# Mixture-of-experts stage on one core: the smallest expert group's rows in four 32-column tiles of TensorE instead of two of 64

## The chip, the core and the metric

The kernel runs on one core of a Trainium2 chip. The metric is the device time of one execution in microseconds. Before the change it is 1832.76 us, the median of 3 runs (1832.09 to 1835.33).

## What is computed

Two layers of a transformer-like trunk over 512 frames of width 1024. Each layer has a mixing half (three kinds of attention between one input and one output projection) and a mixture-of-experts half; the change lies in the second. All of it is float32. The part that matters, cut from the reference:

```python
h2 = rms_norm(x) * (1 + sc2) + sh2            # 512 x 1024
scores = sigmoid(h2 @ router_w)               # 32 experts in 8 groups of 4
g_sel = argmax over groups of (sum of the best two biased scores of a group)
idx, gates = the best two experts inside the group g_sel
for each of a token's two experts e:
    u = silu(h2 @ w_gate[e]) * (h2 @ w_up[e])      # 1024 -> 512
    y += gate * (u @ w_down[e])                    # 512 -> 1024
x = x + gt2 * y
```

A token stays inside one group, so a group is a list of tokens, and each of the 32 experts reads the list of its group. With these inputs the routing formulas put 115, 96, 85, 71, 54, 46, 31 and 14 tokens into the eight groups of the first layer (sorted), and 108, 105, 94, 64, 50, 41, 30 and 20 in the second.

## The kernel before

**Places.** The groups are ranked by count (lines 1276 to 1288). Rank r gets `CAPS[r]` places in a gathered activation `hs` (lines 1363 to 1376): 128 for ranks 0 to 3 ("wide"), 64 for ranks 4 to 7 ("narrow"), 768 in all. A one-hot matrix `Pt` (line 1310) is multiplied with the activations (line 1370, 2 halves of 384 places, 8 slices of the width, 8 matmuls each), and each result goes through DVE (line 1374) or ACT (line 1376) into `hs`. Tokens beyond a group's places would go through a loop behind the stage (lines 1686 on) that is skipped when there are none.

**Weights.** Each expert has 6 MB in fp32 (gate, up and down), fetched by SP in pieces of 1 MB (line 1447) into 8 buffers of 1 MB; a buffer comes free when its last reader is done, and SP, which issues in order, waits for that. 192 such transfers make the stage of one layer.

**Wide experts.** ACT casts each half of a piece to a rounded fp32r high part and DVE subtracts to get the low part (`split`, lines 1415 to 1424). TensorE runs three fp32r matmuls of 512 columns for each product (`three`).

**Narrow experts.** No split: plain fp32 matmuls straight from the fetched piece. An fp32 matmul is two passes on TensorE, each a MATMUL with its weight load. With only 64 rows to produce, `halved` puts the first half of the output columns on array columns 0 to 63 (PSUM partitions 0 to 63) and the second half on 64 to 127; the two column tiles run at the same time. A gate or up part is 8 slices x 2 halves x 256 columns, a down part 4 slices x 2 halves x 512 columns. `up_part` folds the halves back with two DVE operations that read every second element, `turn` transposes.

**Order.** `WHERE` alternates a wide rank and a narrow one, in four quarters: ranks 0 and 4, 1 and 5, 2 and 6, 3 and 7; the last four experts are (3,2), (3,3), (7,2), (7,3). The engines' order is written out (`_Pinned`): gate of expert e+1, with the transposes of expert e in the middle, down of e, up of e+1. ACT's casts are put into its queue up to four half pieces ahead of the matmul that reads them. Behind the last expert of a group its sums are gated with gt2 and scattered back to the 512 rows by matmuls with `PT` and DVE adds into `X` (`add`); `combine` does this in steps between the pieces of the next experts, `combine_last` does it for rank 7 at the end of the stage, with nothing behind it but the next layer's start (squares and row norm), or in the second layer the output's store. For a narrow group `add` reads the two column halves of the sums as two row tiles of 64.

In the trace nearly all of this has line 122, the helper that pins the order; tiles tell the parts apart: `g`, `u` and `y` are the sums of gate, up and down, `R` the fetched piece, `H` its split, `x` a scratch bank.

Of the kernel before, what the change touches and what calls it, by code (L numbers as in the profile page):

```python
# [12 lines left out]
F32R = mybir.dt.float32r  # L13
# [3 lines left out]
OP = mybir.AluOpType  # L17
# [10 lines left out]
START = GV, DQ, DK  # L28

NWIDE = 4  # L30
CAPS = (128,) * NWIDE + (64,) * (NG - NWIDE)
OFFS = tuple(sum(CAPS[:r]) for r in range(NG))
PLACES = sum(CAPS)

# [105 lines left out]
def hybrid_trunk(ctx: ExitStack, tc: tile.TileContext, x, c, positions, w_mod, b_mod, norm1_g, norm2_g, w_in,  # L140
# [228 lines left out]
    for l in range(depth):  # L369
        first = l == 0  # L370
        with ExitStack() as ps:
# [900 lines left out]
            def pt_(shape):  # L1272
                return p3.tile(shape)
# [17 lines left out]
            nth, rk, aw, cap, over, slot = [pt_([128, NT]) for _ in range(6)]  # L1291
            V.tensor_mul(tmp.rearrange("p i g -> p (i g)"), pc[:, 0:NT * NG], gf)
            V.tensor_tensor(tmp2, grp, rank[:, None, :].to_broadcast([128, NT, NG]), op=OP.mult)
            V.tensor_reduce(nth, tmp, axis=AX.X, op=OP.add)
            V.tensor_reduce(rk, tmp2, axis=AX.X, op=OP.add)
            V.tensor_scalar(cap, rk, NWIDE - 0.5, CAPS[-1] - CAPS[0], op0=OP.is_gt, op1=OP.mult)
            V.tensor_scalar(aw, rk, float(NWIDE), 0.0, op0=OP.subtract, op1=OP.max)
            V.tensor_scalar(cap, cap, float(CAPS[0]), None, op0=OP.add)
            V.scalar_tensor_tensor(aw, aw, CAPS[-1] / CAPS[0] - 1.0, rk, op0=OP.mult, op1=OP.add)
# [49 lines left out]
            def pre_done():  # L1349

                spre.close()
                pre.clear()
                wn = after["pool"] = pool(spre, f"wn{l}", "right")
                after["gt2b"] = wn.tile([128, D])
                A.dma_start(after["gt2b"], bcast(mods[l, 5 * D:6 * D], D))
                after["gt2h"] = wn.tile([128, 512])
                for n in range(2):
                    A.dma_start(after["gt2h"][64 * n:64 * n + 64], bcast(mods[l, 5 * D + 512 * n:5 * D + 512 * n + 512], 512, 64))

            def pbank(tag, bufs=1, shape=None):  # L1360
                return pm.tile(shape or [128, 512], tag=tag, bufs=bufs)
# [65 lines left out]
                for n, (x_, w_) in enumerate(((0, 0), (0, 1), (1, 0))):  # L1427
                    T.matmul(out, a[:, x_, ka], hl[:, w_, c0:c0 + 512], start=(start and n == 0), stop=(stop and n == 2))

            def halved(out, a, raw, c0, n, start, stop):  # L1430

                n //= 2
                for h in range(2):
                    T.matmul(out[64 * h:64 * h + 64, 0:n], a, raw[:, c0 + h * n:c0 + (h + 1) * n], start=start, stop=stop)

            ranked = {}

# [35 lines left out]
            def wide(acc, src, e, amid=None):  # L1473

                r = where[e][0]
                for p in range(4):
                    hl = src.get()
                    for k in range(2):
                        start, stop = p == 0 and k == 0, p == 3 and k == 1
                        if r < NWIDE:  # L1480
                            three(acc, xTs[r], 2 * p + k, hl, k * 512, start, stop)
                        else:
                            halved(acc, hs[:, 2 * p + k, OFFS[r]:OFFS[r] + 64], hl, k * 512, 512, start, stop)
                    step()
                    if amid and p == 1:
                        amid()
# [5 lines left out]

            def up_part(src, e, gacc):
                r, j = where[e]
                w = 512 if r < NWIDE else 256
# [12 lines left out]
            def turn(u_, e):  # L1508
                b = pbank("x", 3, [128, 4, 128])
                if where[e][0] < NWIDE:  # L1510
                    for q in range(4):
                        T.transpose(b[:, q], u_[:, q * 128:(q + 1) * 128], ident)
                    uT = wm.tile([128, 2, 4, 128], F32R, tag="euT")
                    A.copy(uT[:, 0], b)
                    V.tensor_sub(uT[:, 1], b, uT[:, 0])
                else:
                    for k in range(2):
                        T.transpose(b[:, k], u_[:, k * 128:(k + 1) * 128], ident)
                    uT = wm.tile([128, 2, 128], tag="euT64")
                    A.copy(uT, b[:, 0:2])  # L1520
                return uT

            def down_part(src, e, uT, ya, amid=None):
                r, j = where[e]
                for k in range(4):
                    hl = src.get()
                    start, stop = j == 0 and k == 0, j == 3 and k == 3
                    if r < NWIDE:
                        for n in range(2):
                            three(ya[:, n], uT, k, hl, n * 512, start, stop)  # L1530
                    else:
                        halved(ya[:, 0], uT[:, k % 2, 64 * (k // 2):64 * (k // 2) + 64], hl, 0, D, start, stop)
                    step()
                    if amid and k == 1:
                        amid()

            def gain_y(ya, n, yf, wide_):
                V.tensor_mul(yf, ya[:, n], after["gt2b"][:, n * 512:(n + 1) * 512] if wide_ else after["gt2h"])
                return yf

            def gated(ya, n, wide_):
                return parts(gain_y(ya, n, after["pool"].tile([128, 512], tag="eyf"), wide_))

            def parts(yf):
                yh = after["pool"].tile([128, 2, 512], F32R, tag="eyh", bufs=2)
                A.copy(yh[:, 0], yf)
                V.tensor_sub(yh[:, 1], yf, yh[:, 0])
                return yh
# [8 lines left out]
            def add(PT, yhs, ns, i):  # L1557

                if len(yhs) == 2:
                    bs = [(n, pbank("x", 3), slice(0, 128), yhs[n]) for n in ns]  # L1560
                else:
                    bs = [(n, pbank("x", 3), slice(64 * n, 64 * n + 64), yhs[0]) for n in ns]
                for m in range(2):
                    for n, b, rows, yh in bs:
                        T.matmul(b, PT[rows, i], yh[rows, m], start=(m == 0), stop=(m == 1))
                for n, b, rows, yh in bs:
                    V.tensor_add(X[:, i, n * 512:(n + 1) * 512], X[:, i, n * 512:(n + 1) * 512], b)

            def combine_last(r, ya):

                wide_ = r < NWIDE
# [3 lines left out]
                yfs = [gain_y(ya, n, wm.tile([128, 512], tag=("es", "eu")[n]), wide_) for n in range(2 if wide_ else 1)]  # L1575
                yhs = [parts(yf) for yf in yfs]
                for i in range(NT):
                    add(PT, yhs, (0, 1), i)
                    if l + 1 < depth:
                        for n in range(2):  # L1580
                            squares(i, n)
                    else:
                        store(i)
                if l + 1 < depth:
                    row_rstd()

            def combine(r, ya):

                PT = back(r)
                yield  # L1590
                yhs = []
                for n in range(2 if r < NWIDE else 1):
                    yhs.append(gated(ya, n, r < NWIDE))
                    yield
                for ns in ((0,), (1,)) if r < NWIDE else ((0, 1),):
                    for i in range(NT):
                        add(PT, yhs, ns, i)
                        yield

            where = WHERE  # L1600
# [85 lines left out]
            with tc.If(nov > 0):  # L1686
# [7 lines left out]
                with tc.For_i(0, NG, 1) as r:  # L1694
                    nb = nc.values_load(nbi[0:1, ds(r, 1)], min_val=0, max_val=NT, skip_runtime_bounds_check_because=bound)
                    with tc.If(nb > 0):
# [3 lines left out]
                        with tc.For_i(0, nb, 1) as j_:  # L1700
# [47 lines left out]
                                            T.matmul(ya[:, n], ub[:, 2 * q + k], raw[:, k * D + n * 512:k * D + n * 512 + 512],  # L1748
                                                     start=(j == 0 and q == 0 and k == 0), stop=(j == 3 and q == 1 and k == 1))
                            for n in range(2):  # L1750
                                yf = gain_y(ya, n, wm.tile([128, 512], tag="es"), True)
# [44 lines left out]
```

## Time and profile before

| | before |
|---|---|
| median of 3 runs | 1832.76 us |
| profiled execution | 1833.86 us |
| its span, first to last instruction | 1832.1 us |
| mean granted TensorE clock | 0.980 |
| PE busy | 1751.1 us (96%) |
| DVE busy | 1113.6 us (61%) |
| ACT busy | 795.5 us (43%) |
| moved by DMA | 512.11 MB, mean 280 GB/s |
| moved from 450 to 960 us (experts of the first layer) | 195.34 MB, mean 383 GB/s |

PE's share is that of modelled, pipelined matmuls and is near its top in every stage, so it doesn't tell a bound; the two expert stages (about 450 to 955 us and 1312 to 1817 us) are the only ones in which DMA runs near its top as well.

### The profile page before, as it was taken

The page shows a single profiled execution, that of the slowest core. Times are in us where ns is not written, and L with a number is a line of the kernel's source. Part 1 is how long each engine was busy: PE and PEld are TensorE (multiplying, and loading weights), DVE is VectorE, ACT ScalarE, POOL GpSimd, SP SyncE. Part 2 cuts the span into 40 slices and gives each one's busy share as a digit, 9 for nine tenths or more (in the row PEclk, how much of TensorE's full clock was granted, in tenths as well). Part 3 has the DMA queues.
Part 4 walks back from the last instruction along what each step waited for, and adds up shares of the span by engine and source line. Part 5 has one row for each costly group of instructions (what it writes and reads, how often), then busy time and mean ns, then how long its engine had stood idle before and what let it go on. Part 6 is the DMA issues. An engine that isn't in the chain of part 4 may idle for free. (4 is left out here: it accounts for less than half of the span.)

```text
span 1832.1 us, 28257 instructions
## 1 busy us (share of the span) xinstructions
PE 1751.1 (96%) x10891; PEld 1252.5 (68%) x10892; DVE 1113.6 (61%) x2004; ACT 795.5 (43%) x1215; POOL 88.9 (5%) x136
## 2 busy tenths in 40 slices
PE   5999999988999999999998999997999999999997
PEld 3866767777665666665748887986866666566673
DVE  4646564366548557566655778647555746756664
ACT  3344442354434443444523554445444344444450
POOL 1010000021000000000000110102000000000000
PEclk9999999998999999999998999998999999999998
DMA  9565547426999999999964211131899999999994
GB/s 329 159 220 181 176 154 227 161 97 267 368 421 374 396 422 365 413 422 355 423 249 141 70 47 47 47 131 47 322 381 421 364 411 422 360 414 416 360 421 180
DMA packets 115617, 512.11 MB, mean 280 GB/s; under 512 B 14978, under 2 KB 42896, under 8 KB 66320
## 3 DMA queue, kind: packets, MB, share of 16 engines
q1 hardware_dynamic: 111952, 504.93, 70.8%
q0 software_dynamic: 1072, 3.32, 0.5%
q10 hardware_dynamic: 2448, 1.94, 0.5%
q8 instruction: 89, 1.46, 0.3%
q14 instruction: 56, 0.46, 0.1%
HBM read 501.73 MB, written 8.42 MB: 278 GB/s over the span
## 5 line engine op out<-in xcount | busy, mean ns | idle before, releaser
L122 DVE TENSOR_TENSOR H<-R,H 128x1024 fp32r<-128x1024 f32 x368 | 431.2, 1219 | 97.6 <-ACT H L122 97.2
L122 ACT CAST H<-R 128x1024 fp32r<-128x1024 f32 x368 | 364.0, 1048 | 45.0 <-DMA R<-in_w_down_dram 27.5
L579 PEld LDWEIGHTS a<-H,u 128*128 128x128 f32 x1728 | 216.5, 190 | 45.0 <-issue 42.0
L579 PE MATMUL a<-H,u 128*128 128x256 f32 x1728 | 245.8, 291 | 0.0
L122 PE MATMUL y<-H,euT 128*128 128x512 f32 x768 | 188.6, 400 | 1.5 <-DVE euT L122 1.5
L122 PE MATMUL g<-H,exT 128*128 128x512 f32 x720 | 183.8, 402 | 0.0
L122 PE MATMUL u<-H,exT 128*128 128x512 f32 x720 | 177.0, 400 | 0.0
L122 PEld LDWEIGHTS y<-H,euT 128*128 128x128 f32 x768 | 141.6, 188 | 46.8 <-ACT H L122 9.2
L122 DVE SCALAR_TENSOR_TENSOR eu<-u,u,es 128x256 f32<-128x256 f32 x92 | 56.9, 672 | 191.5 <-PE u L122 191.5
L122 PEld LDWEIGHTS u<-H,exT 128*128 128x128 f32 x720 | 132.7, 188 | 54.1 <-issue 22.5
L122 PEld LDWEIGHTS g<-H,exT 128*128 128x128 f32 x720 | 131.4, 188 | 36.1 <-issue 8.5
L122 PE MATMUL g<-R,u 128*64 128x256 f32 x1024 | 126.9, 387 | 0.0
L122 PE MATMUL y<-R,euT 128*64 128x512 f32 x512 | 121.3, 602 | 1.1 <-ACT euT L122 1.1
L122 PE MATMUL u<-R,u 128*64 128x256 f32 x1024 | 118.9, 383 | 0.0
L122 DVE TENSOR_TENSOR u<-u,x 128x512 f32<-128x512 f32 x128 | 84.2, 682 | 45.7 <-PE x L122 45.5
L122 ACT COPY euT<-x 128x256 f32<-128x256 f32 x32 | 11.9, 372 | 211.8 <-PE x L122 191.2
L122 PEld LDWEIGHTS u<-R,u 128*64 128x64 f32 x1024 | 70.3, 137 | 45.2 <-issue 13.8
L122 PEld LDWEIGHTS g<-R,u 128*64 128x64 f32 x1024 | 67.0, 136 | 47.7 <-issue 20.6
L122 PE MATMUL x<-eyh,ePT 128*128 128x512 f32 (+1 forms) x256 | 75.5, 464 | 11.1 <-DVE u L122 7.5
L122 ACT CAST euT<-x 128x512 fp32r<-128x512 f32 x32 | 18.7, 584 | 151.5 <-PE x L122 151.5
L122 PEld LDWEIGHTS y<-R,euT 128*64 128x64 f32 x512 | 32.3, 136 | 63.7 <-issue 52.5
L122 PEld LDWEIGHTS x<-eyh,ePT 128*128 128x128 f32 (+1 forms) x256 | 34.0, 194 | 53.2 <-DVE u L122 33.0
(597 smaller groups left out, 2271.7 us busy)
## 6 DMA issues: line engine op xcount, KB each, us to landing
R<-in_w_gate_dram SPq DMA_DIRECT2D x128, 1024.0 KB
R<-in_w_up_dram SPq DMA_DIRECT2D x128, 1024.0 KB
R<-in_w_down_dram SPq DMA_DIRECT2D x128, 1024.0 KB
M<-in_w_mod_dram SPq DMA_DIRECT2D x80, 512.0 KB
R<-in_w_in_dram SPq DMA_DIRECT2D x20, 1024.0 KB
slab<-in_w_mod_dram SPq DMA_DIRECT2D x16, 512.0 KB
R<-in_w_in_dram SPq DMA_DIRECT2D x24, 256.0 KB
R<-in_w_out_dram SPq DMA_DIRECT2D x4, 1024.0 KB
```

The source lines that it names most:

```text
L122: return self.tc.keep_in_program_order(f(*args, **kw))
L579: T.matmul(acc[i // 2][:, i % 2], a[q][:, k, tk], hl[:, w, k], start=(i % 2 == 0 and q == 0 and k == 0 and n3 == 0), stop=(i % 2 == 1 and ...
```

## The change

Rank 7 gets 32 places in place of 64 (736 places in all, halves of 368). Its gate and up products go into four column tiles of 32 with 128 output columns each, its down product into four tiles of 256; the columns of a gate or up tile are every second one of a half of the piece's 512, so that the four tiles hold whole 128-row slices for the transposes. Two transposes turn into one, and two strided DVE products into one plain one. Its sums lie in four row tiles of 32, and the scatter adds 256 columns at a time, in two rounds of two. Two small DVE operations compute the caps, and four small transfers on ACT's queue load a gt2 folded to four quarters. The core of the diff:

```diff
-CAPS = (128,) * NWIDE + (64,) * (NG - NWIDE)
+CAPS = (128,) * NWIDE + (64,) * (NG - NWIDE - 1) + (32,)
...
-            V.tensor_scalar(cap, rk, NWIDE - 0.5, CAPS[-1] - CAPS[0], op0=OP.is_gt, op1=OP.mult)
+            V.tensor_scalar(cap, rk, NWIDE - 0.5, CAPS[NWIDE] - CAPS[0], op0=OP.is_gt, op1=OP.mult)
...
+            V.tensor_scalar(least, rk, NG - 1.5, CAPS[-1] - CAPS[NWIDE], op0=OP.is_gt, op1=OP.mult)
+            V.tensor_add(cap, cap, least)
...
-                for n in range(2):
-                    A.dma_start(after["gt2h"][64 * n:64 * n + 64], bcast(mods[l, 5 * D + 512 * n:5 * D + 512 * n + 512], 512, 64))
+                after["gt2q"] = wn.tile([128, 256])
+                for name, c in (("gt2h", 64), ("gt2q", 32)):
+                    w = D * c // 128
+                    for n in range(128 // c):
+                        o = 5 * D + w * n
+                        A.dma_start(after[name][c * n:c * (n + 1)], bcast(mods[l, o:o + w], w, c))
...
-            def halved(out, a, raw, c0, n, start, stop):
-
-                n //= 2
-                for h in range(2):
-                    T.matmul(out[64 * h:64 * h + 64, 0:n], a, raw[:, c0 + h * n:c0 + (h + 1) * n], start=start, stop=stop)
+            def halved(out, a, cap, columns, start, stop):
+
+                for h, w in enumerate(columns):
+                    T.matmul(out[cap * h:cap * (h + 1), 0:w.shape[-1]], a, w, start=start, stop=stop)
...
-                            halved(acc, hs[:, 2 * p + k, OFFS[r]:OFFS[r] + 64], hl, k * 512, 512, start, stop)
+                            w, cap = hl[:, k * 512:(k + 1) * 512], CAPS[r]
+                            wq = w.rearrange("p (q t k) -> p q k t", q=2, k=2)
+                            halved(acc, hs[:, 2 * p + k, OFFS[r]:OFFS[r] + cap], cap, [w[:, 0:256], w[:, 256:512]] if cap == 64 else
+                                   [wq[:, h // 2, h % 2] for h in range(4)], start, stop)
...
+                if w == 128:
+                    V.scalar_tensor_tensor(u_, acc[:, 0:w], gcs[:, r, j:j + 1], s, op0=OP.mult, op1=OP.mult)
...
-                    for k in range(2):
+                    n = CAPS[where[e][0]] // 32
+                    for k in range(n):
                         T.transpose(b[:, k], u_[:, k * 128:(k + 1) * 128], ident)
...
-                        halved(ya[:, 0], uT[:, k % 2, 64 * (k // 2):64 * (k // 2) + 64], hl, 0, D, start, stop)
+                        cap, w = CAPS[r], D * CAPS[r] // 128
+                        a = uT[:, k % 2, 64 * (k // 2):64 * (k // 2) + 64] if cap == 64 else uT[:, 0, 32 * k:32 * k + 32]
+                        halved(ya[:, 0], a, cap, [hl[:, h * w:(h + 1) * w] for h in range(128 // cap)], start, stop)
...
-                    bs = [(n, pbank("x", 3), slice(64 * n, 64 * n + 64), yhs[0]) for n in ns]
+                    bs = [(n, pbank("x", 3)[:, 0:w], slice(cap * n, cap * n + cap), yhs[0]) for n in ns]
...
-                    V.tensor_add(X[:, i, n * 512:(n + 1) * 512], X[:, i, n * 512:(n + 1) * 512], b)
+                    V.tensor_add(X[:, i, n * w:(n + 1) * w], X[:, i, n * w:(n + 1) * w], b)
+
+            def rounds(r):
+
+                return {128: ((0,), (1,)), 64: ((0, 1),), 32: ((0, 2), (1, 3))}[CAPS[r]]
...
                 for i in range(NT):
-                    add(PT, yhs, (0, 1), i)
+                    for ns in rounds(r):
+                        add(PT, yhs, ns, i, CAPS[r])
```

## Rows read from the trace of the kernel before

**Rows 1.** Windows: stretch and length, busy time by engine, PEclk, DMA share, GB/s.
```profile
842.50:864.00 21.50, 20.53 (x116) 13.66 (x114) 15.29 (x17) 10.52 (x13) 0.00 (x0) 1.00 0.89 336
864.00:936.00 72.00, 72.00 (x384) 49.45 (x381) 45.49 (x48) 33.03 (x40) 0.00 (x0) 1.00 1.00 413
1705.00:1728.00 23.00, 22.03 (x126) 14.29 (x124) 16.77 (x19) 11.20 (x14) 0.00 (x0) 1.00 0.89 332
1728.00:1798.00 70.00, 70.00 (x376) 48.58 (x374) 44.09 (x47) 32.12 (x38) 0.00 (x0) 1.00 1.00 415
```

**Rows 2.** DMA view, 924 to 944 us, then 1786 to 1806 us: GB/s in 40 slices.
```profile
GB/s 426 426 410 377 393 426 442 426 393 492 393 410 442 426 442 410 360 410 360 393 410 360 328 344 426 393 475 279 115 49 33 0 0 0 0 33 0 0 0 109
...
GB/s 426 377 475 426 393 459 426 426 442 360 475 442 393 442 442 410 442 393 426 410 393 442 360 442 344 344 426 377 442 213 98 33 0 0 0 0 0 0 0 0
```

**Rows 3.** Timeline of PE, ends of both expert stages: start, us, instructions, idle before.
```profile
882.20 3.67 PE L122 MATMUL u<-R,u 128*64 128x256 f32 x32
885.81 3.07 PE L122 MATMUL g<-H,exT 128*128 128x512 f32 x12
...
891.82 3.65 PE L122 MATMUL y<-R,euT 128*64 128x512 f32 x16
895.41 5.86 PE L122 MATMUL u<-H,exT 128*128 128x512 f32 x24
...
950.27 3.65 PE L122 MATMUL y<-R,euT 128*64 128x512 f32 x16 [0.53 <-ACT euT L122]
...
1813.28 3.65 PE L122 MATMUL y<-R,euT 128*64 128x512 f32 x16 [0.53 <-ACT euT L122]
```

**Rows 4.** Page, part 5: the narrow experts' gate and down matmuls, both layers.
```profile
L122 PE MATMUL g<-R,u 128*64 128x256 f32 x1024 | 126.9, 387 | 0.0
L122 PE MATMUL y<-R,euT 128*64 128x512 f32 x512 | 121.3, 602 | 1.1 <-ACT euT L122 1.1
```

**Rows 5.** Timeline of PE, attention stage: matmuls in four column tiles of 32.
```profile
119.97 0.62 PE L695 MATMUL l<-QF,KF 128*32 128x128 f32 x16
120.41 0.40 PE L322 MATMUL m<-M,u 128*32 128x256 f32 x4
...
173.25 1.07 PE L322 MATMUL m<-M,u 128*32 128x256 f32 x16
```

**Rows 6.** Waits of SP, 842.5 to 864 us: total, times, longest.
```profile
SPq L1447 <- PE g L122: 9.2, 2, 8.2
SPq L1447 <- PE u L122: 5.7, 2, 4.5
```

**Rows 7.** Timeline of DVE, end of the second layer: gating and adds of rank 7.
```profile
1816.98 0.69 DVE L122 TENSOR_TENSOR es<-y,u 128x512 f32<-128x512 f32 x1 [7.09 <-PE y L122]
...
1819.82 1.28 DVE L122 TENSOR_TENSOR u<-u,x 128x512 f32<-128x512 f32 x2 [0.78 <-PE x L122]
1821.40 1.28 DVE L122 TENSOR_TENSOR u<-u,x 128x512 f32<-128x512 f32 x2 [0.30 <-PE x L122]
```

**Rows 8.** Timeline of ACT: gt2 loads, next operation; the next layer's first cast.
```profile
466.90 1.68 ACTq L122 DMA_DIRECT2D u<-u  x3
468.63 0.39 ACT L122 ACTIVATE es<-g 128x256 f32<-128x256 f32 x1 [0.74 <-DVE H L122]
...
951.53 0.83 ACT L500 CAST H<-R 128x768 fp32r<-128x768 f32 x1
```

**Rows 9.** Timeline of DVE: evictions into hs, and two routing operations.
```profile
443.36 0.68 DVE L1374 TENSOR_SCALAR u<-x,u 128x384 f32<-128x384 f32 x1 [2.10 <-PE x L1370]
446.14 0.68 DVE L1374 TENSOR_SCALAR u<-x,u 128x384 f32<-128x384 f32 x1 [2.10 <-PE x L1370]
...
419.51 0.15 DVE L1298 TENSOR_SCALAR u<-u 128x4 f32<-128x4 f32 x1
419.58 0.15 DVE L1299 SCALAR_TENSOR_TENSOR u<-u,u 128x4 f32<-128x4 f32 x1
```

**Rows 10.** Timeline of DVE: a wide expert's two products that read every second element.
```profile
918.55 1.18 DVE L122 SCALAR_TENSOR_TENSOR eu<-u,u,es 128x256 f32<-128x256 f32 x2 [5.54 <-PE u L122]
```

**Rows 11.** Windows with a fallen clock (columns as in Rows 1).
```profile
30.70:37.50 6.80, 6.09 (x31) 5.06 (x32) 5.47 (x7) 3.00 (x4) 0.00 (x0) 0.50 1.06 397
957.00:977.00 20.00, 11.21 (x47) 8.91 (x48) 13.80 (x26) 10.53 (x24) 3.23 (x6) 0.57 0.62 210
```

More of the change, by code (lines that the diff above doesn't have):

```diff
@@ L1290, in hybrid_trunk @@
             tmp, tmp2 = pt_([128, NT, NG]), pt_([128, NT, NG])
-            nth, rk, aw, cap, over, slot = [pt_([128, NT]) for _ in range(6)]
+            nth, rk, aw, cap, over, slot, least = [pt_([128, NT]) for _ in range(7)]
             V.tensor_mul(tmp.rearrange("p i g -> p (i g)"), pc[:, 0:NT * NG], gf)
@@ L1295, in hybrid_trunk @@
             V.tensor_reduce(rk, tmp2, axis=AX.X, op=OP.add)
-            V.tensor_scalar(cap, rk, NWIDE - 0.5, CAPS[-1] - CAPS[0], op0=OP.is_gt, op1=OP.mult)
+            V.tensor_scalar(cap, rk, NWIDE - 0.5, CAPS[NWIDE] - CAPS[0], op0=OP.is_gt, op1=OP.mult)
             V.tensor_scalar(aw, rk, float(NWIDE), 0.0, op0=OP.subtract, op1=OP.max)
             V.tensor_scalar(cap, cap, float(CAPS[0]), None, op0=OP.add)
-            V.scalar_tensor_tensor(aw, aw, CAPS[-1] / CAPS[0] - 1.0, rk, op0=OP.mult, op1=OP.add)
+            V.tensor_scalar(least, rk, NG - 1.5, CAPS[-1] - CAPS[NWIDE], op0=OP.is_gt, op1=OP.mult)
+            V.tensor_add(cap, cap, least)
+            V.scalar_tensor_tensor(aw, aw, CAPS[NWIDE] / CAPS[0] - 1.0, rk, op0=OP.mult, op1=OP.add)
             V.tensor_tensor(over, nth, cap, op=OP.is_ge)
@@ L1494, in up_part @@
                 r, j = where[e]
-                w = 512 if r < NWIDE else 256
+                w = FE * CAPS[r] // 128
                 s = wm.tile([128, FE], tag="es")[:, 0:w]
@@ L1516, in turn @@
                 else:
-                    for k in range(2):
+                    n = CAPS[where[e][0]] // 32
+                    for k in range(n):
                         T.transpose(b[:, k], u_[:, k * 128:(k + 1) * 128], ident)
                     uT = wm.tile([128, 2, 128], tag="euT64")
-                    A.copy(uT, b[:, 0:2])
+                    A.copy(uT[:, 0:n], b[:, 0:n])
                 return uT
@@ L1535, in down_part, with gain_y, gated @@
                         amid()
[L1537 to L1542, printed above, removed]
+            def gain_y(ya, n, yf, r):
+                w = min(512, D * CAPS[r] // 128)
+                g_ = {128: "gt2b", 64: "gt2h", 32: "gt2q"}[CAPS[r]]
+                V.tensor_mul(yf[:, 0:w], ya[:, n, 0:w], after[g_][:, n * 512:n * 512 + w])
+                return yf[:, 0:w]
+            def gated(ya, n, r):
+                return parts(gain_y(ya, n, after["pool"].tile([128, 512], tag="eyf"), r))
             def parts(yf):
-                yh = after["pool"].tile([128, 2, 512], F32R, tag="eyh", bufs=2)
+                yh = after["pool"].tile([128, 2, 512], F32R, tag="eyh", bufs=2)[:, :, 0:yf.shape[-1]]
                 A.copy(yh[:, 0], yf)
@@ L1555, in squares, with add @@
                              accum_out=sums[:, i, n:n + 1])
-            def add(PT, yhs, ns, i):
-                if len(yhs) == 2:
+            def add(PT, yhs, ns, i, cap):
+                w = min(512, D * cap // 128)
+                if cap == 128:
                     bs = [(n, pbank("x", 3), slice(0, 128), yhs[n]) for n in ns]
                 else:
-                    bs = [(n, pbank("x", 3), slice(64 * n, 64 * n + 64), yhs[0]) for n in ns]
+                    bs = [(n, pbank("x", 3)[:, 0:w], slice(cap * n, cap * n + cap), yhs[0]) for n in ns]
                 for m in range(2):
@@ L1566, in add @@
                 for n, b, rows, yh in bs:
-                    V.tensor_add(X[:, i, n * 512:(n + 1) * 512], X[:, i, n * 512:(n + 1) * 512], b)
+                    V.tensor_add(X[:, i, n * w:(n + 1) * w], X[:, i, n * w:(n + 1) * w], b)
+            def rounds(r):
+                return {128: ((0,), (1,)), 64: ((0, 1),), 32: ((0, 2), (1, 3))}[CAPS[r]]
             def combine_last(r, ya):
-                wide_ = r < NWIDE
                 if l + 1 < depth:
@@ L1574, in combine_last @@
                 PT = back(r)
-                yfs = [gain_y(ya, n, wm.tile([128, 512], tag=("es", "eu")[n]), wide_) for n in range(2 if wide_ else 1)]
+                yfs = [gain_y(ya, n, wm.tile([128, 512], tag=("es", "eu")[n]), r) for n in range(2 if r < NWIDE else 1)]
                 yhs = [parts(yf) for yf in yfs]
                 for i in range(NT):
-                    add(PT, yhs, (0, 1), i)
+                    for ns in rounds(r):
+                        add(PT, yhs, ns, i, CAPS[r])
                     if l + 1 < depth:
@@ L1592, in combine @@
                 for n in range(2 if r < NWIDE else 1):
-                    yhs.append(gated(ya, n, r < NWIDE))
+                    yhs.append(gated(ya, n, r))
                     yield
-                for ns in ((0,), (1,)) if r < NWIDE else ((0, 1),):
+                for ns in rounds(r):
                     for i in range(NT):
-                        add(PT, yhs, ns, i)
+                        add(PT, yhs, ns, i, CAPS[r])
                         yield
@@ L1750, in hybrid_trunk @@
                             for n in range(2):
-                                yf = gain_y(ya, n, wm.tile([128, 512], tag="es"), True)
+                                yf = gain_y(ya, n, wm.tile([128, 512], tag="es"), 0)
                                 for i in range(NT):
```

## The prediction

> **What bounds the kernel now.** The page's slices show two things that no other stage has together: in the expert stages PE and DMA are both near their tops. Which of them ends last has to be read in the quarter where rank 7 works, the last of each layer, so I cut it by windows. From 842.5 to 864 us the transfers run at 336 GB/s, from there to 936 us at 413 GB/s with a DMA share of 1.00; in the second layer it is 332 and then 415 [rows 1]. PE is busy throughout. The waits of SP tell why the first stretch is slow: it waits for PE to free buffers, 8.2 us in one case [rows 6]. So PE holds the transfers back up to 864 us, and from there both run side by side, DMA without a pause.
>
> Then I looked where each one ends. The DMA slices (0.5 us each) fall to nothing at about 939.5 us, and at 1802.0 us in the second layer [rows 2]. The last matmuls of the stage end at 953.9 and 1816.9 us, 14.4 and 14.9 us later [rows 3]. PE works off pieces that have long landed. A faster PE can gain that tail, plus what it hands the transfers as earlier buffers; more it can't.
>
> **The change, part by part.** The sum is made against the profiled execution (1833.86 us, span 1832.1); the median of the runs shown is 1.1 us lower, and the last step takes that off.
>
> *Rank 7's matmuls.* An up part of 64 rows takes 3.61 us from its start to the next part's (882.20 to 885.81), a down part 3.59 us [rows 3]; the totals over all narrow experts agree (126.9 us for 32 gate parts is 3.97 us, with other work in between) [rows 4]. The attention stage has the new shape: sixteen matmuls of 32 rows and 128 columns from 119.97 us on let the next start at 120.41, so four tiles with 128 columns take 0.11 us a pass; with 256 columns it is (1.07-0.40)/3 = 0.22 us [rows 5]. A gate or up part becomes 16 passes x 0.11 = 1.76 us, a down part 8 x 0.22 = 1.76 us; with the 0.15 us that the present part has above its pure passes, 1.9 us. Each saves 1.7 us, twelve parts 20.4 us of PE per layer.
>
> The new gate and up columns are every second float of a piece, and no matmul of the trace reads so. The nearest row is on DVE: two products of 256 elements that read every second one take 1.18 us [rows 10], as long as two plain ones of 512 (1.28 us) [rows 7], so twice the price for an element. I take no extra cost, because the fp32 pass wants a column only every 0.86 ns (0.11 us for 128), while the wide experts' matmuls read 512 floats in 5.86/24 = 0.24 us, one every 0.48 ns [rows 3]: every second float at the fp32 pace passes over floats about as fast. But I keep twice (0.22 us a pass) and four times as bounds. The Trainium skill's page "Advanced Engine Details and Errata", section "SBUF Cachelines", says that reads run at full rate as long as two hits fall on a line of 16 bytes, which a step of 8 bytes still does. By it the parts stay at 1.9 us; by the DVE row gate and up would gain nothing, and the time would be 1820 us. The DVE row has one operand in PSUM, so it doesn't decide.
>
> *What of the 20.4 us reaches the end.* Transfers at share 1.00 can't come earlier by anything that PE does. Before 864 us the stretch of 21.5 us lost 21.5 x (1-336/413) = 4.0 us to the waits, in the second layer 23 x (1-332/415) = 4.6 us [rows 1]. The waits for PE's gate and up parts are what rank 7's shorter parts cut; I take 3.5 us in each layer, bounds 0 and 5.5 (a little of the stretch before also counts). The last transfer then lands at 936.0 and 1798.5 us. Behind it come the last two slices of the last down part, 0.9 us, their semaphores, and about 0.9 us more because PE, waiting for each piece, may be at the lower clock by then: 2.0 us (bounds 1 and 3.5). The last matmul ends at 938.0 in place of 953.9, and at 1800.5 in place of 1816.9: **-15.9 and -16.4 us**. By PE's work alone the ends would be 933.5 and 1796.5, so PE is ahead of the transfers by some 4 us and waits for them; its wide parts, whose casts ACT does in order only after landing, are where it waits.
>
> *The last scatter (`combine_last`), on the path in both layers.* Gating, cast and subtraction of 256 columns in place of 512 start the first matmul about 0.8 us earlier. Eight adds of 512 become sixteen of 256. One add of 512 takes 0.69 us, two 1.28, and the next pair starts 1.58 us after the last (1819.82 to 1821.40), 0.3 of it waiting for PE [rows 7]. An add of 256 has half the columns and the same fixed part, about 0.42 us, 0.33 behind another; a round of two is 0.66 plus a wait of about 0.35 us for the matmuls, because three scratch banks let only part of the next round run ahead. Eight rounds of 1.0 in place of four of 1.58 us: +1.7, less 0.8: **+1.0 us** in the second layer. In the first, the squares of a row block follow its last add, now both late: **+1.6 us**. Bounds -0.8 and +4 each.
>
> *The next layer's first cast.* ACT has it in its queue ahead of the scatter's cast (951.53 us) [rows 8], and its weights are fetched behind the last expert piece. They now land about when the cast is wanted: **+0.7 us** in the first layer, bounds 0 and 2.
>
> *Places.* 368 columns in place of 384 save 4% of the gather: two evictions every 2.78 us [rows 9], 8 times a layer, 22 us x 4% = -0.85 us. The two new DVE operations step at 0.07 us [rows 9], +0.14 us. **-0.7 us a layer.** It lies ahead of all expert work and passes through.
>
> *Costs at nothing.* Four gt2 loads are issued on ACT: three such take 1.68 us now [rows 8], so about 2.2 us more. What queues behind is one Silu (468.63 us), read only after the next up part, and casts for a part after that; PE has the down and up part between to work on. Without that cover it would be 2.2 us per layer. One transpose and one 256-element product less per expert lie under the transfers. The routing's counts (14 and 20 tokens) fit 32 places, so the loop behind the stage stays skipped.
>
> *Sum:* -15.9 - 16.4 + 1.0 + 1.6 + 0.7 - 1.4 = -30.4; 1833.9 - 30.4 = 1803.5, and against the median **1802.4 us**. With the bounds of the terms 1796 to 1810.
>
> **The rivals.**
>
> *The transfers follow PE.* If earlier buffers let DMA regain all it lost before, PE's 20.4 us a layer count in full: -40.8 + 2.6 - 1.4, about 1793 us. For it: DMA waits for PE up to 864 us. Against: 413 GB/s at share 1.00 afterwards, which leaves only about 5 us to regain.
>
> *The clock falls.* With the transfers as bound PE waits in short pieces. The granted clock fell to 1.2 GHz around stretches in which PE had little to do: 957 to 977 us, busy 11.2 of 20 us, mean 0.57 [rows 11]; it stayed at 2.4 GHz from 842.5 to 864 us, which holds a wait of 0.97 us [rows 1]. A fallen stretch lasted 6.8 us at least [rows 11], which costs 3.4 us of work. Three or four of them in the last quarter cost 12 us; less the 4.6 us by which PE is ahead, each layer loses 7.4 us of the gain: 1817 us. [...] The rows bear it out only for longer lulls, and the waits here come to 1 to 2 us at a time, so I give it less.
>
> *Strided columns at half rate.* Only the down parts gain: 6.8 us a layer, PE stays the bound, -13.6 + 2.6 - 1.4: 1820 us.
>
> *Slower: strided columns at a quarter of the rate.* A gate or up part takes 16 x 0.44 + 0.15 = 7.2 us in place of 3.6, eight parts +28.8 us, down -6.8: +22 a layer, about 1878 us. It turns slower from 0.26 us a pass. For it speaks only the DVE row, and it would have to be doubled.
>
> *It doesn't do what it says: the four tiles go two and two.* Then parts keep their length, and the scatter's +2.6 and -1.4 are left: 1834 us. Against it: 0.11 us a pass for four tiles [rows 5].
>
> **How the numbers follow.** Forecast 0.58; transfers follow 0.10; clock 0.13; half rate 0.08; quarter rate 0.05; two and two 0.06. The range from 1792 to 1819 holds the first three, 0.81. A measurement of this kernel can tell about 0.2% (3.7 us) from no change. Faster: 0.58+0.10+0.13+0.08 = 0.89; same 0.06; slower 0.05.
>
> **What the changed profile would show.** Rank 7's up part at about 1.9 us; DMA share 1.00 to the end of the last quarter and the last landing within 3 us of the last expert matmul; PE's idle time in that quarter up from almost none to some 5 us per layer, ended by casts or by landings; sixteen adds of about 0.4 us in rounds of about 1.0 us. Wrong would be: parts of 3.6 us (columns or tiles), a granted clock under 1.00 from 864 to 930 us (clock), or a matmul end that stays 10 us behind the last landing.

## The result: 1.1% faster, and where it fell short of the forecast

| | before | after |
|---|---|---|
| median of 5 runs each | 1832.76 us | 1812.01 us (1810.68 to 1816.36) |
| ratio | | 0.9887, 95% interval 0.9872 to 0.9903 |
| profiled execution | 1833.86 us | 1812.01 us |
| its span | 1832.1 us | 1810.3 us |
| mean granted clock | 0.980 | 0.977 |

The forecast was 1802.4 us with a range of 1792 to 1819. The sign and the bound came out as predicted and the time lies in the range, but the size is short: the profiled executions differ by 21.9 us where the sum had 30.4.

### The profile after

The timeline of PE in the kernel after, at the places of [rows 3] (start, us, instructions, idle before), with the four places where the text below needs it:

```profile
477.09 0.51 PE L122 MATMUL g<-H,exT 128*128 128x512 f32 x1 [0.69 <-ACT H L122]
478.35 2.82 PE L122 MATMUL g<-H,exT 128*128 128x512 f32 x11 [0.76 <-DVE H L122]
482.33 0.44 PE L122 MATMUL x<-u,eu 128*128 128x128 f32 x2 [1.16 <-DVE eu L122]
485.49 3.65 PE L122 MATMUL y<-R,euT 128*64 128x512 f32 x16
...
843.31 0.66 PE L122 MATMUL g<-R,u 128*32 128x128 f32 x16
843.91 0.50 PE L122 MATMUL x<-eyh,ePT 64*128 64x512 f32 x1
845.98 0.87 PE L122 MATMUL x<-eyh,ePT 64*128 64x512 f32 x3 [1.58 <-DVE u L122]
...
880.42 2.04 PE L122 MATMUL u<-R,u 128*32 128x128 f32 x64
882.39 3.07 PE L122 MATMUL g<-H,exT 128*128 128x512 f32 x12
888.29 1.94 PE L122 MATMUL y<-R,euT 128*32 128x256 f32 x32
...
939.88 1.07 PE L122 MATMUL y<-R,euT 128*32 128x256 f32 x16 [0.48 <-DMA R<-in_w_down_dram]
941.93 0.85 PE L122 MATMUL x<-eyh,ePT 32*128 32x256 f32 x5 [0.98 <-ACT eyh L122]
...
1793.18 1.07 PE L122 MATMUL y<-R,euT 128*32 128x256 f32 x16 [0.27 <-DMA R<-in_w_down_dram]
```

An up part now takes 1.97 us (880.42 to 882.39) instead of 3.61. The last down matmuls of both layers, which in [rows 3] waited for `euT`, now wait for the transfer of their own piece. They end at 940.95 and 1794.25 us, and by the records of the transfers' packets the last weight lands at 939.34 and 1792.69: 1.6 us from the last landing to the last matmul, where it was 14.3 and 14.9 before. PE's surplus is used up, and the transfers set the end.

Windows of the kernel after (columns as in [rows 1]). The first four answer to those rows; the first, third and fourth lie as far behind the start of the last quarter as there. The others are single stretches:

```profile
844.30:865.80 21.50, 19.92 (x188) 14.56 (x188) 16.32 (x18) 10.99 (x14) 0.00 (x0) 0.92 0.92 343
864.00:936.00 72.00, 70.32 (x670) 51.11 (x666) 48.85 (x56) 33.96 (x42) 0.00 (x0) 1.00 1.01 421
1697.10:1720.10 23.00, 21.42 (x198) 15.69 (x193) 17.45 (x19) 10.99 (x14) 0.00 (x0) 0.93 0.91 338
1720.10:1789.30 69.20, 67.19 (x637) 49.07 (x639) 46.12 (x52) 32.85 (x40) 0.00 (x0) 1.00 1.01 422
842.00:846.40 4.40, 2.82 (x40) 1.53 (x32) 4.40 (x7) 0.00 (x0) 0.00 (x0) 1.00 0.64 233
846.40:849.90 3.50, 3.50 (x40) 2.28 (x38) 3.46 (x6) 1.97 (x3) 0.00 (x0) 0.51 0.84 309
1699.80:1703.20 3.40, 3.40 (x38) 2.41 (x38) 3.40 (x5) 2.10 (x3) 0.00 (x0) 0.50 0.81 272
1303.80:1307.20 3.40, 3.40 (x10) 2.62 (x9) 3.40 (x4) 1.41 (x2) 0.00 (x0) 0.50 0.99 419
```

From 864 us on DMA runs without a pause, as before, and PE idles for 1.7 of 72 us. The first stretch is hardly better than before (343 GB/s against 336, in the second layer 338 against 332): at 842 to 846.4 us DVE is busy for all 4.40 us, PE waits for it, and right behind that the clock is at 1.2 GHz (0.51) for 3.5 us, in the second layer (0.50) for 3.4.

The cost of the change shows on ACT, at the place of [rows 8]. Timeline of ACT after, first and second layer (ACTq is its queue issuing DMAs):

```profile
466.76 8.91 ACTq L122 DMA_DIRECT2D u<-u  x7
475.72 0.38 ACT L122 ACTIVATE es<-g 128x256 f32<-128x256 f32 x1 [7.97 <-DMA u<-u]
...
1320.41 8.05 ACTq L122 DMA_DIRECT2D u<-u  x7
1328.51 0.38 ACT L122 ACTIVATE es<-g 128x256 f32<-128x256 f32 x1 [7.10 <-DMA u<-u]
```

Seven issues take 8.9 us where three took 1.68. ACT's next operation is put down to a landing of one of these transfers (`<-DMA u<-u`), not to the length of the issues: ACT was idle for 8.0 and 7.1 us. The same lines of the first layer in narrower windows show where:

```profile
466.76 3.47 ACTq L122 DMA_DIRECT2D u<-u  x6
...
475.37 0.31 ACTq L122 DMA_DIRECT2D u<-u  x1
```

Six loads are issued in 3.47 us, 0.58 us each, and the seventh only 5.1 us later. The trace's records of the semaphores tell why: the loads and SP's transfers take eight DMA semaphores in turn, the seventh load has the one of the first (a load of 512 KB, issued at 466.76 us), and its issue waits until that one has landed. In the second layer it is the same pair. So ACT stands for a landing that the program itself asks for; no record shows a full queue.

PE's lines of 477 to 485 us above are what follows: it waits for casts, for the subtractions behind them and for the Silu's product, and the second expert's down part (the expectation of experiment 1 calls it the third's) starts at 485.49 us, in the kernel before at 482.59.

Timeline of DVE after, the last scatter, at the place of [rows 7]; first layer, then second:

```profile
942.81 0.75 DVE L122 TENSOR_TENSOR u<-u,x 128x256 f32<-128x256 f32 x2 [0.47 <-PE x L122]
943.48 0.95 DVE L501 TENSOR_TENSOR H<-R,H 128x768 fp32r<-128x768 f32 x1
944.35 0.75 DVE L122 TENSOR_TENSOR u<-u,x 128x256 f32<-128x256 f32 x2
...
1794.32 0.42 DVE L122 TENSOR_TENSOR es<-y,u 128x256 f32<-128x256 f32 x1 [4.16 <-PE y L122]
...
1799.92 0.75 DVE L122 TENSOR_TENSOR u<-u,x 128x256 f32<-128x256 f32 x2 [0.35 <-PE x L122]
1801.01 0.75 DVE L122 TENSOR_TENSOR u<-u,x 128x256 f32<-128x256 f32 x2 [0.34 <-PE x L122]
```

The later rounds take 1.10 us (1799.92 to 1801.01), 0.35 of it waiting for PE; all eight start within 7.10 us, 1.01 us apart on average. In the first layer subtractions for the next layer (L501) stand between the first rounds, which come every 1.53 us.

So the 21.9 us divide as follows. The start of the quarter is rank 3's up part ahead of rank 7's first gate part (832.74 before, 834.53 after; 1695.71 and 1687.80).

| us | first layer: predicted | measured | second layer: predicted | measured |
|---|---|---|---|---|
| up to the last quarter | -0.7 | +1.8 | -0.7 | +2.0 |
| last quarter, to the last expert matmul | -15.9 | -14.8 | -16.4 | -14.8 |
| behind it (scatter, next cast) | +2.3 | +3.0 | +1.0 | +0.9 |
| sum | -14.3 | -10.0 | -16.1 | -11.9 |

### The profile page after: what moved, and what is told of

It is laid out like the page before. It is cut to its first block, busy times and chain, and to the rows that moved or that the text cites. A ratio compares the mean times of both kernels' runs of the same rounds, so it can differ in the third digit from the quotient of the medians.

```text
span 1810.3 us, 29627 instructions
## 1 busy us (share of the span) xinstructions
PE 1715.6 (95%) x11563; PEld 1246.0 (69%) x11564; DVE 1110.1 (61%) x2024; ACT 794.3 (44%) x1215; POOL 89.4 (5%) x136
## 5 line engine op out<-in xcount | busy, mean ns | idle before, releaser
L122 DVE SCALAR_TENSOR_TENSOR eu<-u,u,es 128x256 f32<-128x256 f32 (+1 forms) x92 | 54.2, 642 | 170.2 <-PE u L122 170.2
L122 PE MATMUL g<-R,u 128*64 128x256 f32 (+1 forms) x1280 | 115.2, 350 | 0.0
L122 DVE TENSOR_TENSOR u<-u,x 128x512 f32<-128x512 f32 (+1 forms) x144 | 85.7, 622 | 39.6 <-PE x L122 39.1
L122 PE MATMUL y<-R,euT 128*64 128x512 f32 (+1 forms) x640 | 107.9, 515 | 1.6 <-ACT euT L122 0.9
L122 PE MATMUL u<-R,u 128*64 128x256 f32 (+1 forms) x1280 | 105.7, 341 | 0.0
L122 PEld LDWEIGHTS g<-R,u 128*64 128x64 f32 (+1 forms) x1280 | 64.6, 128 | 42.0 <-issue 20.5
L122 PEld LDWEIGHTS u<-R,u 128*64 128x64 f32 (+1 forms) x1280 | 66.7, 125 | 37.7 <-issue 13.5
L122 PE MATMUL x<-eyh,ePT 128*128 128x512 f32 (+2 forms) x288 | 78.8, 443 | 14.0 <-DVE u L122 11.9
L122 PEld LDWEIGHTS x<-eyh,ePT 128*128 128x128 f32 (+2 forms) x288 | 38.1, 199 | 51.9 <-DVE u L122 33.4
L122 PEld LDWEIGHTS y<-R,euT 128*64 128x64 f32 (+1 forms) x640 | 31.1, 125 | 54.7 <-issue 41.0
```

The lines of the kernel that those rows point to most:

```text
L122: return self.tc.keep_in_program_order(f(*args, **kw))
```

## The experiments

Which of the lost microseconds are the gt2 loads', which the transfers', the scatter's and the clock's? Expectations are quoted as written before each run. The kernel before was run again beside each group and had medians of 1833.2 to 1833.6 us.

### 1. The two folded tiles with one transfer each

```diff
-                    for n in range(128 // c):
-                        o = 5 * D + w * n
-                        A.dma_start(after[name][c * n:c * (n + 1)], bcast(mods[l, o:o + w], w, c))
+                    A.dma_start(after[name],
+                                bass.AP(tensor=gt2.tensor, offset=gt2.offset, ap=[[w, 128 // c], [0, c], [1, w]]))
```

> The changed kernel, but the two folded gt2 tiles are loaded by one transfer each, so that ACT issues three small transfers there as before, in place of seven. Theory A (the seventh issue on ACT's queue waits for an earlier transfer to land, ACT stands for 8 us behind it, and the casts queued there are late): the stand goes, and 2.9 us in the first layer and 2.3 us in the second come back, so about 1807 us; the down part of the third expert starts as early against the kernel before as the parts ahead of it. Theory B (the loss at that place comes from something else, such as the new bytes in a full DMA queue): still about 1812 us.

Measured: 1815.21 us, ratio 0.9901 (0.9888 to 0.9915), no faster than the change itself. The stand on ACT was gone, but something else came. DMA view from 455 to 500 us (GB/s in 40 slices of 1.1 us, then the queue of the small transfers: packets, MB, share), joined:

```profile
GB/s 371 401 437 437 408 430 131 0 160 393 357 127 299 415 412 248 65 209 346 333 320 386 381 418 382 429 414 378 378 413 377 356 127 68 53 80 211 422 393 430
...
q10 hardware_dynamic: 406, 0.92, 6.4%
```

and the kernel after in the same stretch:

```profile
GB/s 240 269 408 422 430 401 444 284 36 80 342 408 273 277 415 351 264 200 157 364 408 291 379 350 350 400 328 430 371 211 408 422 422 437 415 430 437 415 277 386
...
q10 hardware_dynamic: 496, 0.92, 8.0%
```

The same bytes come in 90 packets fewer. 384 of the packets carry the data; the rest are one end mark for each DMA engine that a transfer uses: 112 after, that is seven transfers on 16 engines, and 22 joined, that is 16 for the untouched transfer and 2 and 4 for the joined ones. The Trainium skill's page "DMA: Bandwidth & Descriptors", section "Rules for kernel authors", says that an outermost dimension of fewer than 16 confines a transfer to at most that many engines; the joined sources have outermost dimensions of 2 and 4, and the trace agrees. With the same bytes on so few engines the small transfers lasted 26.6 us (467.3 to 493.9) instead of 10.6. From 491 to 495 us DMA moved only 53 to 127 GB/s, because SP had issued nothing since 483.8 us: its next weight transfer takes a semaphore that one of the small transfers held. Waits of SP in that run, 483 to 496 us (total, times, longest):

```profile
SPq L1452 <- DMA u<-u: 11.4, 2, 10.5
```

SP issued again at 494.44 us, when the last small one had landed. What that cost shows later, on ACT, which in the kernel after doesn't wait there:

```profile
530.43 1.99 ACT L122 CAST H<-R 128x1024 fp32r<-128x1024 f32 x2 [5.07 <-DMA R<-in_w_gate_dram]
560.17 1.99 ACT L122 CAST H<-R 128x1024 fp32r<-128x1024 f32 x2 [4.95 <-DMA R<-in_w_gate_dram]
```

PE lost about 5 us in the first layer in this way and about 2 in the second. So the run removed one cost and put another of the same kind in its place; by its time alone it decides nothing on the stand.

### 2. The four quarter loads on POOL's queue

```diff
-                        A.dma_start(after[name][c * n:c * (n + 1)], bcast(mods[l, o:o + w], w, c))
+                        (A if c == 64 else G).dma_start(after[name][c * n:c * (n + 1)], bcast(mods[l, o:o + w], w, c))
```

First a single execution, then five.

> The changed kernel, but the four loads of the quarter-folded gt2 are issued on POOL's queue, which is idle there; ACT keeps its three. Theory A (ACT's queue stands): about 1807 us, like the joined loads. Theory B (the bytes or small packets of the loads): about 1812 us, since the same four transfers still run at the same place.

> The version with the four quarter loads on POOL's queue, timed. Theory A (the stand of ACT's queue is what the loads cost): 1807 us within 2, that is 5 us below the changed kernel, and no idle time of ACT behind the loads over 1 us in either layer.

Measured: 1807.29 us in the single execution, then 1805.58 (1805.16 to 1808.0), ratio 0.9849 (0.9836 to 0.9863). The same four loads, the same bytes, another queue: 6.4 us less by the medians, 4.0 between the profiled executions. Timeline of ACT, first layer:

```profile
466.58 1.69 ACTq L122 DMA_DIRECT2D u<-u  x3
468.31 0.39 ACT L122 ACTIVATE es<-g 128x256 f32<-128x256 f32 x1 [0.75 <-DVE H L122]
```

The Silu is back at 468.31 us. In the kernel after, the second expert's down part was 2.9 us behind the kernel before; here it starts at 482.18 us, 0.4 ahead. So the cost of the loads is the stand of ACT's queue, not their bytes. POOL's queue takes its loads as 64 packets of 2 KB where ACT's took 128 of 1 KB, and on semaphores of its own; this run alone doesn't part the packets and the queue from the semaphore, but the records above do.

### 3. The loads alone, in the kernel before

```diff
+                after["gt2q"] = wn.tile([128, 256])
+                for n in range(4):
+                    A.dma_start(after["gt2q"][32 * n:32 * n + 32], bcast(mods[l, 5 * D + 256 * n:5 * D + 256 * n + 256], 256, 32))
```

> The kernel before, with nothing of the change but the four extra gt2 loads on ACT's queue (nothing reads them). Theory A: ACT stands for about 8 us behind the seventh issue and the time rises by 5 us, to about 1838 us. Theory B (the loss needs the new places or shapes): within 1 us of the kernel before.

Measured: 1835.27 us in a single execution, against 1833.63 before (1830.2 to 1835.32). That is less than expected, and the time alone tells nothing; the trace does. Timeline of ACT, both layers:

```profile
467.10 6.03 ACTq L122 DMA_DIRECT2D u<-u  x7
473.17 0.38 ACT L122 ACTIVATE es<-g 128x256 f32<-128x256 f32 x1 [5.09 <-DMA u<-u]
...
1330.02 7.52 ACTq L122 DMA_DIRECT2D u<-u  x7
1337.59 0.38 ACT L122 ACTIVATE es<-g 128x256 f32<-128x256 f32 x1 [6.58 <-DMA u<-u]
```

The stand comes back, but shorter; again the seventh issue waits for the landing of the first. Followed from the second expert's up part to its down part against the kernel before, 5.09 us of it cost PE 0.14 us, and 6.58 us cost 1.64. In the kernel after 7.10 us cost 2.3 and 7.97 cost 3.1. In all four the cost is the stand less about 4.9 us: that much is covered by PE's other work, and only what goes beyond it counts. The cover that the prediction named is real and was too small for what it had to hide.

### 4. Less and more work for PE in rank 7

Is PE or DMA the bound at the end? Two kernels change PE's work alone. The first leaves out every second slice of rank 7's gate and up products (on the base of experiment 1), the second computes them twice (on the base of experiment 2):

```diff
-                    for k in range(2):
-                        start, stop = p == 0 and k == 0, p == 3 and k == 1
+                    for k in range(2 if CAPS[r] > 32 else 1):
+                        start, stop = p == 0 and k == 0, p == 3 and (k == 1 or CAPS[r] == 32)
```

> The joined version, and rank 7's gate and up parts leave out every second of the eight slices of the width (the weights are all still fetched), so each of these parts is some 0.9 us shorter, 7 us of PE per layer. Theory C (in the last quarter the transfers set the end, PE waits for them): the time stays within 2 us of the joined version, and PE's idle time in the quarter grows by the 7 us. Theory D (PE still sets it): 12 to 14 us less than the joined version.

```diff
+                            for t in range(1 if cap == 64 else 2):
+                                halved(acc, hs[:, 2 * p + k, OFFS[r]:OFFS[r] + cap], cap, cols,
+                                       start and t == 0, stop and (cap == 64 or t == 1))
```

> The POOL version, and every gate and up matmul of rank 7 runs twice into the same sum (a doubled product), 1.75 us more in each of eight parts, 14 us of PE per layer. Theory C (transfers set the end of the last quarter and PE has idle time of 4 to 5 us there): the idle time goes, the rest shows: 9 to 10 us a layer, 1826 us, and PE ends well behind the last landing again. Theory D (PE sets it already, idle time is no slack): 28 us more, 1835 us.

Measured: half the work 1814.07 us in a single execution, against 1812.46 of its base's profiled execution and 1815.21 of its median: nothing gained. Twice the work 1823.33 us, also in one, 17.7 above its base's median. Windows and last down matmuls, first the kernel with half the work (the last line is the window of its last down matmuls):

```profile
864.00:936.00 72.00, 66.75 (x490) 45.67 (x486) 49.13 (x56) 34.17 (x43) 0.00 (x0) 1.00 1.01 422
...
940.83 1.93 PE L122 MATMUL y<-R,euT 128*32 128x256 f32 x16 [1.34 <-DMA R<-in_w_down_dram]
...
940.80:942.80 2.00, 1.93 (x16) 0.59 (x16) 0.00 (x0) 0.00 (x0) 0.00 (x0) 0.52 1.04 363
```

then with twice:

```profile
864.00:936.00 72.00, 72.00 (x892) 57.06 (x893) 45.23 (x49) 32.62 (x40) 0.00 (x0) 1.00 1.01 420
...
944.82 1.93 PE L122 MATMUL y<-R,euT 128*32 128x256 f32 x32 [0.44 <-ACT euT L122]
```

Half the work turns into idle time of PE (5.3 of 72 us, 2.3 in its base), and the last matmul waits for its piece as before. Behind that wait of 1.34 us it runs at 1.2 GHz (0.52) and takes 1.93 us where the kernel after took 1.07. With twice the work PE is never idle, the transfers keep their 420 GB/s, and the last matmul waits for `euT` again; it ends 9 us behind the last landing. So the change has brought PE's work in rank 7 to just below what the transfers allow, and less of it gives nothing more.

### 5. Five banks for the last scatter

`add` rotates over three scratch banks. At the end of the stage the banks of gate and up are idle, so this kernel (on the base of experiment 2) lets rank 7's scatter rotate over five:

```diff
+            def bank_of(cap):
+
+                turns_[0] += cap == 32
+                k = turns_[0] % 5
+                return pbank("x", 3) if cap != 32 or k < 3 else pbank("gu"[k - 3])
...
-                    bs = [(n, pbank("x", 3)[:, 0:w], slice(cap * n, cap * n + cap), yhs[0]) for n in ns]
+                    bs = [(n, bank_of(cap)[:, 0:w], slice(cap * n, cap * n + cap), yhs[0]) for n in ns]
```

> The POOL version, and the last scatter of rank 7 takes its sums in turn from five scratch banks (the three of before and the two of the gate and up sums, free by then). Theory F (the scatter's eight rounds of about 1.1 us hold 0.35 us of waiting for a bank each): the rounds fall to about 0.75 us and each layer ends about 2.5 us earlier, 1802 us. Theory G (the rounds are bound by the sixteen adds or by the matmuls at the low clock): within 1 us of the POOL version.

Measured: **1800.43 us** (1798.62 to 1803.68), ratio 0.982 (0.9807 to 0.9833). Timeline of DVE, second layer, first and last lines of the adds into x banks:

```profile
1790.23 0.75 DVE L122 TENSOR_TENSOR u<-u,x 128x256 f32<-128x256 f32 x2 [0.47 <-PE x L122]
1791.56 1.08 DVE L122 TENSOR_TENSOR u<-u,x 128x256 f32<-128x256 f32 x3
1793.22 1.08 DVE L122 TENSOR_TENSOR u<-u,x 128x256 f32<-128x256 f32 x3
1794.87 0.74 DVE L122 TENSOR_TENSOR u<-u,x 128x256 f32<-128x256 f32 x2
```

No add after the first waits for PE. From the first add to the end of the last it is 5.39 us in both layers, 8.45 in the second layer of experiment 2 and 9.74 in its first. The first layer's 4.35 us, though, don't reach the next layer. Timeline of DVE there:

```profile
944.79 1.82 DVE L501 TENSOR_TENSOR H<-R,H 128x768 fp32r<-128x768 f32 x2
...
953.38 0.48 DVE L429 TENSOR_SCALAR at<-u,u 128x128 f32<-128x128 f32 x2 [3.67 <-SPq L1715]
```

The next layer's subtractions have moved behind the adds; SP issues the next fetch of `w_in` at 946.64 us, when they are done (942.51 in experiment 2), and everybody waits for SP at the skipped loop, DVE 3.67 us. PE's transposes of the next layer start at 953.72 us, in experiment 2 at 953.77. Of the 5.2 us between the medians of this run and of experiment 2 the second layer's adds show 3.1. What the rest is the traces don't show: the profiled executions, 4.3 us apart, differ besides by a fallen stretch of the clock at the second layer's first gate part, which experiment 2's has and this one's doesn't. The first layer's 4 us are still there for an order that frees SP earlier; that was not tried.

### 6. Rank 6 at 32 places too, alone and with the five banks

Rank 6 has 31 and 30 tokens, so it fits 32 places as well. On the base of experiment 2, then with the banks of experiment 5 for the last scatter alone:

```diff
-CAPS = (128,) * NWIDE + (64,) * (NG - NWIDE - 1) + (32,)
+CAPS = (128,) * NWIDE + (64,) * (NG - NWIDE - 2) + (32,) * 2
...
-            V.tensor_scalar(least, rk, NG - 1.5, CAPS[-1] - CAPS[NWIDE], op0=OP.is_gt, op1=OP.mult)
+            V.tensor_scalar(least, rk, NG - 2.5, CAPS[-1] - CAPS[NWIDE], op0=OP.is_gt, op1=OP.mult)
...
+            V.tensor_scalar(least, rk, NG - 1.5, (CAPS[-1] - CAPS[NWIDE]) / CAPS[0], op0=OP.is_gt, op1=OP.mult)
+            V.tensor_add(aw, aw, least)
```

> The POOL version, and rank 6 gets 32 places as well (its 31 and 30 tokens fit), so that the third quarter loses 20 us of PE work per layer too. Theory C (transfers become the bound wherever PE gets this short; what PE lagged behind them can be gained only once): 3 to 6 us a layer, 1795 to 1801 us. Theory D (the stage goes as PE's work goes): 15 us or more a layer, 1777 us or less.

> The five-bank version and 32 places for rank 6 as well. Theory C (transfers set both quarters, what PE lagged is gained once): what the second narrow rank brought alone, 2 us, comes on top of the five banks, 1797 to 1800 us, with the last landing of the first layer where it was (936 us). Theory H (the fallen clock that the second narrow rank showed in the third and fourth quarter eats what it gains): within 1 us of the five-bank version, 1800 us.

Measured: 1803.53 us (1802.7 to 1805.61), ratio 0.984 (0.9827 to 0.9854), 2 us below its base and less than theory C had; with the banks 1800.18 us (1797.44 to 1800.53), ratio 0.9814 (0.98 to 0.9827), the same as the banks alone. The work of PE that was taken out is there, and doesn't reach the end. Windows of 700 to 850 us, where rank 6 works, with both:

```profile
700.00:850.00 150.00, 136.03 (x1141) 93.84 (x1140) 98.94 (x123) 64.71 (x79) 0.00 (x0) 0.95 0.98 401
```

and with the five banks alone:

```profile
700.00:850.00 150.00, 146.81 (x805) 93.82 (x806) 100.74 (x116) 63.73 (x79) 0.00 (x0) 0.99 0.96 389
```

PE idles for 14 us instead of 3, DMA goes from a share of 0.96 to 0.98, and the clock from a mean of 0.99 to 0.95. The first layer's last weight lands when it did (935.84 us in experiment 2, 935.38 here), and in the second layer it is 490.4 us from the first gate part to the last matmul, 491.0 with the banks alone. Whether the transfers alone hold the end there, or the fallen clock takes a part of it, the runs don't separate.

## Why the prediction was right in its bound and short in its size

**Rank 7's matmuls: right.** 1.97 us for an up part and 1.86 for a down part stand against 1.9. The strided columns cost nothing, so both rivals on them are out, and so is the one in which the tiles go two and two. The Trainium skill's "SBUF Cachelines" (page "Advanced Engine Details and Errata") said so, and the trace agrees: sixteen passes of 128 columns, eight bytes apart, in 1.97 us.

**Transfers as the bound at the end: right.** "PE is ahead of the transfers by some 4 us and waits for them" holds: the last matmul follows the last landing by 1.6 us (predicted 2.0), and experiment 4 shows it from both sides. PE's idle time in the last quarter was forecast at some 5 us; from 842.5 us to the last matmul it is 4.2, of which 1.6 is the wait for DVE at 844 us.

**"I take 3.5 us in each layer": too large.** The quarter gained 14.8 us in each layer and not 15.9 and 16.4. Counted from its start the last weight lands 2.1 and 1.5 us earlier than before, and the first stretch still runs at 343 and 338 GB/s. Rank 7's first gate part is where PE was to become faster, and there the scatter of rank 6 stands between its matmuls; the trace shows PE waiting for DVE (1.58 us, in both layers) and DVE busy throughout. A shorter part gains nothing where DVE is the bound. The clock's fall behind that wait costs up to 1.7 us more.

**"Costs at nothing. Four gt2 loads are issued on ACT": the step that failed.** It priced four issues by the three in [rows 8], at 0.56 us each, and covered 2.2 us with PE's down and up part. The price of an issue holds (0.58 us for each of six). What the sum lacked is a wait: the trace of before had seven in a row nowhere, and the seventh is issued only when the first has landed, whose semaphore it takes. The seven took 8 to 9 us, and the cover was 4.9 us. Cost: 3.1 us in the first layer and 2.3 in the second; experiment 2 takes it away by another queue (-6.4 us of the median, -4.0 between the profiled executions) and experiment 3 puts a shorter stand into the kernel before. This is the largest part of the missing 8.5 us.

**The last scatter and the next cast: right in the second layer, small in the first.** +0.9 us against +1.0: the rounds come every 1.01 us on average, where 1.0 was taken, and the first add starts 1.0 us earlier behind the last matmul, where 0.8 was. In the first layer +3.0 against 2.3: the prediction had both rounds and the next layer's cast, but not DVE's subtractions behind that cast, which stand between the adds.

**Places:** -0.4 and -0.9 us against -0.7 each. Behind them the gates of rank 7 go to four tiles instead of two, and the small matmuls between the first gate part's cost 0.3 us more in each layer, which the sum lacked.

**The clock.** The rival had three or four fallen stretches in the last quarter. There was one in each layer, of about 3.4 us, and it came behind PE's wait for DVE, not behind waits for transfers: from 864 to 936 us the granted clock is 1.00 with PE waiting in pieces. The Trainium skill's page "TensorE: Matmul & The Clock Gate", section "HAM oscillation", describes a kernel whose bursts are shorter than the waits for DMA between them, and each burst starts at the low clock. The waits of this trace from 864 to 936 us are 0.4 to 0.6 us, far shorter than the work between them, and it shows no low clock there. That a wait for a transfer can do it shows in experiment 4, with half the work. One more stretch fell at 1303.8 us, in the second layer's first gate part, behind matmuls with 4 rows or columns. It cost 1.5 us: the same 21 matmuls take 6.70 us there and 5.15 in experiment 1. The profiled executions of experiment 2 and of the half-work kernel have it too; those of the kernel before, of experiments 1, 3, 5 and 6 and of the kernel with twice the work don't. What decides it stays open.

**The bounds.** "With the bounds of the terms 1796 to 1810" is not the sum of these bounds, which is 1791.5 to 1819; the measured time lies outside the one and inside the other.

What stays open: the wide parts of the first three quarters, which the change doesn't touch, go about 0.05 us faster each, some 1 us in each layer. It is in the first row of the table above and has no shown cause.

## What to carry to other kernels

Where two resources run side by side, find the end of each: what the faster one can gain is the distance between the ends and no more, and more work taken out of it turns into idle time. Price an added DMA issue by more than its issue time: look which earlier transfer it has to wait for (here the one whose semaphore it takes) and who stands behind it, and move setup loads to an engine that nobody waits for. When a long stage becomes shorter, look at the small serial piece behind it: the last scatter of the second layer gave back 3 us for two idle banks.

## What the runs showed of the hardware beyond what was expected

- Three loads in a row on ACT took 1.7 us to issue and six 3.5. A seventh, on the semaphore of the first, was issued only when the first had landed; seven took 6.0 to 8.9 us and left ACT idle for 5.1 to 8.0.
- Joined loads with source patterns of 2 and 4 outer steps used 2 and 4 DMA engines by their end marks, took 26.6 us instead of 10.6, and held back the weights: SP waited 10.5 us for a landing among them before it issued the next one.
- Waits of PE of 0.4 to 0.6 us, and with half the work of up to 0.95 us, left the clock at 2.4 GHz over 72 us. After a stretch of 4.4 us with PE busy for 2.82 it fell to 1.2 GHz for about 3.4 us, and with half the work after one of 3.8 us with PE busy for 1.74.
